# Three projections of a mixer and a cross attention: the last k-group of each pair of column blocks by seven products

## The chip, the cores and the metric

One program runs on one core of a Trainium2 chip. The metric is the device time of one execution in microseconds (us), the median of several runs. The engines are named as the profile names them: PE is TensorE (matmuls and transposes), DVE VectorE, ACT ScalarE, POOL GpSimd, and SP is SyncE, whose one queue issues the DMAs.

## What is computed

The input is 256 rows of width D = 2048 in fp32, which pass through two blocks. The first is a sliding-window attention and a gated feed-forward layer (FFN). The second block, where the change lies, is a hybrid mixer, a cross attention to 256 rows of memory, and an FFN with a short convolution, and then a last norm. Cut to the parts that matter:

```python
def hybrid_mixer(h, w_in, w_a2, b_a, g_gla, w_pool, pool_scale, w_branch, w_out):
    proj = h @ w_in                       # q, k, v, r, (gate rank 16), p, two gates of 2048
    ...
    o = gla_chunked(q, k, v, log_a)       # causal, with decays from the rank-16 gate
    ...
    o_gla = o.astype(h.dtype) * jax.nn.silu(r)
    o_pool = multiscale_pool(p, w_pool, pool_scale)
    y_gla = o_gla @ w_branch[:GLA_DV]
    y_pool = o_pool @ w_branch[GLA_DV:]
    gates = jax.nn.sigmoid(proj[..., OFF_G:])
    merged = gates[..., :D_MODEL] * y_gla + gates[..., D_MODEL:] * y_pool
    return merged @ w_out

def memory_cross_attention(h, mem_n, w_cq, w_ckv, w_co):
    q = (h @ w_cq).reshape(B, T, 4, 512)
    kv = (mem_n @ w_ckv).reshape(B, M, 2, 4, 512)
    s = jnp.einsum('bthd,bmhd->bhtm', q, k) * (512 ** -0.5)
    pr = jax.nn.softmax(s, axis=-1)
    return jnp.einsum('bhtm,bmhd->bthd', pr, v).reshape(B, T, D) @ w_co
```

Each of these products keeps nearly fp32 accuracy: a value x is split into a high part and the rest, and a product is the sum of three matmuls (high by high, high by low, low by high).

## The kernel before

**Tiles.** The activations lie transposed in SBUF in four groups of 512 channels, so one k-group is 4 slices of 128 channels by 256 rows, as a high and a low tile. The weights come in units of 512 by 512, 1 MB each, by one DMA on SP's queue (L215, four `raw` buffers). A unit is used as two *tasks*, each half of its rows: ACT casts the half into `wh` (L235), and DVE subtracts that from `raw` into `wl` (L236). There are five `wh` and five `wl` buffers, and `task()` lets the split run three tasks ahead of the matmuls. The order of all units is fixed by `plan()`. A `raw` buffer is loaded anew when the two tasks of its unit are split.

**Matmuls.** `gemm` walks over column blocks and k-groups. For one k and one of two row tiles t it issues the three matmuls of `mm` (L280 to L282), each 128 by 512, into one bank of PSUM. A pair of column blocks has four such banks (two blocks, two row tiles), and one k-group of it is 4 k x 2 blocks x 2 row tiles x 3 = 48 matmuls. PSUM has four banks `acc`, three `aux` and one `po`.

**Seven products.** The FFNs use `pair`, which does one k-group of a pair of blocks by seven products instead of eight: the 2 by 2 block of halves of the weights is combined by four additions on DVE (`form`, L252 to L256), the activations have sums made once, and each product is one task of 2 x 3 = 6 matmuls. A group is then 42 matmuls and seven tasks (seven casts on ACT, seven subtractions on DVE) instead of 48 and four. After the last group, eight additions on DVE and one copy on ACT put the results together, and between any two of the seven products `tick()` may let other work in.

**Order.** PE runs exactly in the order in which the code issues its work. The orders of DVE, ACT and SP are made by a scheduler, and each engine then works through its list from the front. Everything small (transposes, softmax, the GLA and pooling work) is written as generators, *jobs*: `spawn` starts one, `tick()`, called after each k of a `gemm`, steps each of them, and a `yield n` in a job makes it wait for n ticks. `need(job)` runs a job to its end at once. So a job's matmuls stand between those of the projections, some ticks behind the point where its input was made.

**The stages of the change.** The mixer projects 16 column blocks of `w_in`, in order q, k (`head_job`), then v, the pooling input (`pool_job`), r (`gla_out_job`), and then gates in turn with `w_br`. `gla_job` loads `w_a` for the rank-16 gate (L902), casts it (L904), multiplies (L917), and computes the GLA decays level by level on DVE (L955 to L971). `gla_out_job` takes a bank for each row tile, squares on ACT, a power on POOL (L445) and scales on DVE (L1026). In the cross attention, a job `memory` loads and norms the memory (squares at L1086) during the four blocks of `w_cq`. Then for each of four heads `w_ckv` gives K in one block and V in the next: `on_k` scales K (L436) and spawns a `group_job`, which three ticks later transposes it (L421) and splits the result (L403 on ACT, L404 on DVE). `on_v` scales V (L1102, L1103) and spawns `cross_job`, which does the scores, the softmax and the product with V. At its start stand the lines

```python
qT, kT = self.need(qT), self.need(kT)
S = self.bank((128, 2, 256))
```

Of the kernel before, what the change touches and what calls it, by code (L numbers as in the profile page):

```python
# [83 lines left out]
class _Net:  # L84
# [87 lines left out]
    def plan(self):  # L172

        p, U = [], self.units
        self.seven = set()

        def add(chunks, late=False):
            p.extend(chunks[c][g] for c, g in self.order(chunks, late))

        def pair(a, b, seven):  # L180
            for g in range(len(a)):
                if g in seven:
                    self.seven.add(len(p))
# [15 lines left out]
        add([U("w_in", n) for n in (0, 1)], True)  # L199
        add([U("w_in", n) for n in (2, 3, 6, 7, 4, 5)])  # L200
        for ns in BRANCH:
            add([U("w_in", 8 + 4 * j + n) for n in ns for j in range(2)])
            add([U("w_br", n, (2 * j, 2 * j + 1)) for n in ns for j in range(2)])
        add([U("w_out", n) for n in range(4)], True)
        add([U("w_cq", n) for n in range(4)], True)
        add([U("w_ckv", 4 * j + h) for h in range(4) for j in range(2)])
# [94 lines left out]
    def differences(self, acts, seven):  # L301


        nc = self.nc
        out = []
        for g, z in enumerate(acts):
            h, l = z = self.need(z)
            f = self.s4([128, 4, 256])
            nc.vector.tensor_add(f, h.bitcast(F32), l.bitcast(F32))
            p, q = f[:, :, 0:128], f[:, :, 128:256]  # L310
            yield 2
            if g not in seven:
                h, l = (self.s2([128, 4, 128], F32R) for _ in range(2))
                nc.vector.tensor_sub(p, p, q)
                nc.scalar.copy(h, p)
                nc.vector.tensor_sub(l, p, h.bitcast(F32))
            else:
                s = self.s4([128, 8, 128])
                nc.vector.tensor_add(s[:, 0:2], q[:, 0:2], q[:, 2:4])
                nc.vector.tensor_sub(s[:, 2:4], s[:, 0:2], p[:, 0:2])  # L320
                nc.vector.tensor_sub(s[:, 4:6], p[:, 0:2], q[:, 0:2])
                nc.vector.tensor_sub(s[:, 6:8], p[:, 2:4], s[:, 2:4])
                yield 1
                h, l = (self.s4([128, 8, 128], F32R) for _ in range(2))
                nc.scalar.copy(h, s)
                nc.vector.tensor_sub(l, s, h.bitcast(F32))
            out.append((h, l))
            yield 2
        return out

    def pair(self, left, right, acts, diffs, seven):
# [18 lines left out]
        o1 = None  # L350
        for g in range(len(acts)):
# [14 lines left out]
            end = g == seven[-1]  # L366
            product(p3, S, 6, 0, end)
            product(o1, A, 0, 0, end)
# [4 lines left out]
            if end:  # L373
                add(a, p2, u)
                yield a
            product(o6, S, 2, 0, end)
            if end:
                add(u, o6, u)
            product(p5, S, 0, 0, end)
# [4 lines left out]
            product(o7, S, 4, 0, end)  # L384
            if end:
# [440 lines left out]
    def mixer(self):  # L826
# [4 lines left out]

        def proj(c, done):
            return (self.units("w_in", c), done)

        def head_job(pss, sc):

            rows = self.scaled(pss, sc)
            yield 4
            dst = self.s4([128, 2, 4, 128])
            for t in range(2):  # L840
                b = self.bank((128, 4, 128))
                for h in range(4):
                    nc.tensor.transpose(b[:, h], rows[t][:, h * 128:h * 128 + 128], self.ident)
                nc.scalar.copy(dst[:, t], b)
                yield 1
            return dst

        qk = []
        self.gemm([proj(0, lambda p: qk.append(self.spawn(head_job(p, rq)))),
                   proj(1, lambda p: qk.append(self.spawn(head_job(p, r))))], xacts, late=True)  # L850
        gla = self.spawn(self.gla_job(xacts, r, qk))
# [8 lines left out]
        def on_r(p):  # L860
            t = self.s4([128, 2, 512])
            for i in range(2):
# [4 lines left out]

        self.gemm([proj(2 + c, on_v) for c in range(2)], xacts)
        self.gemm([proj(6 + c, lambda p, c=c: pacts.append(self.spawn(self.pool_job(c, p, r)))) for c in range(2)],
                  xacts)  # L870
        self.gemm([proj(4 + c, on_r) for c in range(2)], xacts)

        macts, gates = [], {}

        def on_gate(p, n, j):
            for t in range(2):
                s = gates[n, j, t] = self.s2([128, 512])
                nc.scalar.activation(s, p[t], AF.Sigmoid, scale=r[:, t:t + 1])

# [8 lines left out]
        for ns in BRANCH:  # L888
            self.gemm([proj(8 + 4 * j + n, lambda p, n=n, j=j: on_gate(p, n, j))
                       for n in ns for j in range(2)], xacts)  # L890
            for n in ns:
# [5 lines left out]
    def gla_job(self, xacts, r, qk):  # L897
# [22 lines left out]
        aT = self.s2([32, 256])  # L920
        nc.vector.tensor_copy(aT, pa)
        yield 1
        bT = self.s4([128, 2, 4, 128])
        z, e = self.s4([128, 2, 512]), self.s4([128, 2, 512])
        for t in range(2):
            pz = self.bank()
            nc.tensor.matmul(pz, aT[:, t * 128:t * 128 + 128], wa2, start=True, stop=True)
            nc.vector.scalar_tensor_tensor(z[:, t], pz, r[:, t:t + 1], ba, op0=ALU.mult, op1=ALU.add)

        nc.scalar.activation(e, z, AF.Abs)  # L930
# [5 lines left out]
        for t in range(2):  # L936
            b = self.bank((128, 4, 128))
            for h in range(4):
                nc.tensor.matmul(b[:, h], z[:, t, h * 128:h * 128 + 128], self.tri, start=True, stop=True)
            nc.scalar.copy(bT[:, t], b)  # L940
            yield 1
        qT, kT = (self.need(z) for z in qk)
# [60 lines left out]
    def gla_out_job(self, c, gla, v, sr):  # L1003
# [5 lines left out]
        for t in range(2):  # L1009
# [18 lines left out]
            og.append(o)  # L1028
            yield 1
        hl = yield from self.group_job(og, self.gains("g_gla_2", c))  # L1030
        return hl

    def pool_job(self, c, pss, r):
# [19 lines left out]
        for g in range(2):
            b = self.bank((128, 2, 256))
            for dt in range(2):
                for ct in range(2):
                    nc.tensor.matmul(b[:, dt], wpl[:, g, ct, dt * 128:dt * 128 + 128], pooled[:, g, ct],
                                     start=ct == 0, stop=ct == 1)
            self.split(hl, 2 * g, b, self.gains("pool_scale_2", c))
            yield 1  # L1060
        return hl


    def cross(self):
# [7 lines left out]
        def memory():  # L1072
# [7 lines left out]
            for t in range(2):  # L1080
# [4 lines left out]
                for i, raw in enumerate(raws):  # L1085
# [4 lines left out]
        rm = self.spawn(memory())  # L1090
        self.gemm([(self.units("w_cq", n),
                    lambda p: qT.append(self.spawn(self.group_job(self.scaled(p, rq))))) for n in range(4)], xacts, late=True)
        rm = self.need(rm)

        def on_k(p):
            kT.append(self.spawn(self.group_job(self.scaled(p, rm))))
# [10 lines left out]

        self.gemm([(self.units("w_ckv", 4 * j + h), f)
                   for h in range(4) for j, f in enumerate((on_k, on_v))], macts)
        self.residual("w_co", range(4), oacts, "g_ffn_2", late=True)  # L1110

    def cross_job(self, qT, kT, v):
# [3 lines left out]
        for t in range(2):  # L1116
            for k in range(4):
                self.mm(S[:, t], qT, k, t, [z[:, k] for z in kT], k == 0, k == 3)
            yield 1
        mx, den = self.sm([128, 2]), self.sm([128, 2])  # L1120
# [5 lines left out]
        for t in range(2):  # L1126
            nc.vector.tensor_scalar(p[:, t], p[:, t], den[:, t:t + 1], None, op0=ALU.mult)
        yield 3
        b = self.bank((128, 2, 256))
# [3 lines left out]
        pt = self.s2([128, 2, 256], F32R), self.s2([128, 2, 256], F32R)  # L1133
        self.split(pt, 0, b)
        yield 2
        hl = self.group()
        for k in (0, 2):
            b = self.bank((128, 2, 256))
            for j in range(2):
                for m in range(2):  # L1140
                    self.mm(b[:, j], v, m, k + j, [z[:, m] for z in pt], m == 0, m == 1)
            self.split(hl, k, b)
            yield 1
        return hl
# [187 lines left out]
```

## Time and profile before

| | |
|---|---|
| time before, median of 3 runs | 2688.29 us (2687.02 to 2688.56) |
| the profiled execution: its own time | 2686.66 us |
| its span in the trace | 2684.5 us |
| busy: PE, DVE, ACT | 2657.9, 1890.7, 1424.2 us |
| granted clock, mean over the span | 0.999 |
| first loads of w_in, w_br, w_out | at 954.5, 1220.8 and 1440.2 us |
| first loads of w_cq, w_ckv, w_co | at 1531.0, 1623.3 and 1819.5 us |
| K and V of the first head scaled | at 1672.37 and 1695.01 us |

The span is the time from the first to the last record, and the profiled execution's own time is 2.2 us longer. All times in rows are counted from the span's start. A matmul's record (0.39 us) is longer than the distance to the next one, since they overlap. So the distance of starts is what one costs.

### The profile page before, as it was taken

To read this page: it belongs to the slowest core of one execution; us is meant where nothing else is said; L and a number is where in the kernel's file an instruction comes from. 1 tells how busy PE (TensorE), PEld (TensorE's weight loads), DVE (VectorE), ACT (ScalarE), POOL (GpSimd) and SP (SyncE) were. 2 spreads that over 40 slices of the span, in tenths; PEclk is the share of its full clock that TensorE was granted. 3 is DMA by queue.
4 is the path that set the end of the run, shared out by engine and by line. 5 is a ranking of instruction groups with operands and counts; after the bars stand their busy time and mean duration, and the time that the engine had idled before them with its cause. 6 is when DMAs were issued, how large, how long until landed. Compare 5 with 4: busy or idle time off the path is not lost.

```text
span 2684.5 us, 31592 instructions
## 1 busy us (share of the span) xinstructions
PE 2657.9 (99%) x12352; PEld 2195.2 (82%) x12352; DVE 1890.7 (70%) x2225; ACT 1424.2 (53%) x1849; POOL 27.1 (1%) x27
## 2 busy tenths in 40 slices
PE   8999999999999999999999999999999999999998
PEld 7778888888888888888888888888878888888887
DVE  7775799888888864655545555454578877777776
ACT  6555555555555555454444555444555655555554
POOL 0100000000000000000000000000000000000000
PEclk9999999999999999999999999999999999999999
DMA  7334455555555554445555566444554555555553
GB/s 304 113 126 145 169 218 187 205 192 206 209 195 200 194 187 178 151 172 188 188 190 193 183 225 212 172 157 168 183 180 175 190 193 194 192 190 195 194 193 138
DMA packets 74086, 499.61 MB, mean 186 GB/s; under 512 B 8496, under 2 KB 9392, under 8 KB 14928
## 3 DMA queue, kind: packets, MB, share of 16 engines
q1 hardware_dynamic: 73936, 497.59, 51.4%
q8 instruction: 97, 1.59, 0.2%
q14 instruction: 53, 0.43, 0.0%
HBM read 495.46 MB, written 2.10 MB: 185 GB/s over the span
## 4 chain that ended last, share of the span: by engine, by line
PE 97%; DVE 2%; ACT 1%; POOL 0%; DMA 0%; issue 0%; SPq 0%; POOLq 0%; DVEq 0%; ACTq 0%
PE acc L280 29%; PE acc L282 29%; PE acc L281 29%; PE aux L421 2%; PE aux L282 1%; PE aux L281 1%; PE aux L280 1%; PE po L734 1%; PE po L282 1%; PE po L281 1%; PE po L280 1%; PE aux L969 0%; POOL sm L445 0%; DVE wl L236 0%; DMA raw<-in_w_qkv 0%; PE aux L695 0%
## 5 line engine op out<-in xcount | busy, mean ns | idle before, releaser
L236 DVE TENSOR_TENSOR wl<-raw,wh 128x1024 fp32r<-128x1024 f32 (+1 forms) x1012 | 1230.7, 1220 | 689.0 <-ACT wh L235 677.1
L235 ACT CAST wh<-raw 128x1024 fp32r<-128x1024 f32 (+1 forms) x1012 | 1060.2, 1051 | 1084.0 <-PE acc L282 1020.6
L280 PE MATMUL acc<-wh,s 128*128 128x512 f32 x3440 | 1364.1, 397 | 7.4 <-ACT wh L235 5.5
L282 PE MATMUL acc<-wh,s 128*128 128x512 f32 x3440 | 1342.6, 390 | 0.6 <-DVE s L404 0.6
L281 PE MATMUL acc<-wl,s 128*128 128x512 f32 x3440 | 1341.0, 390 | 0.4 <-DVE wl L236 0.4
L280 PEld LDWEIGHTS acc<-wh,s 128*128 128x128 f32 x3440 | 646.9, 188 | 145.5 <-DVE s L382 7.1
L282 PEld LDWEIGHTS acc<-wh,s 128*128 128x128 f32 x3440 | 646.2, 188 | 138.1 <-DVE s L404 1.1
L281 PEld LDWEIGHTS acc<-wl,s 128*128 128x128 f32 x3440 | 647.3, 188 | 128.2 <-DVE wl L236 1.7
L467 DVE TENSOR_TENSOR x<-acc,x 128x512 f32<-128x512 f32 x112 | 72.8, 682 | 0.0
L421 PEld LDWEIGHTS aux<-con,s 128*128 128x128 f32 x408 | 50.2, 140 | 15.7 <-issue 4.0
L421 PE MATMUL aux<-con,s 128*128 128x128 f32 x408 | 60.9, 272 | 1.8 <-DVE s L1162 1.8
L1159 ACT ACTIVATE s<-aux,vec 128x256 f32<-128x256 f32 x88 | 47.9, 560 | 12.5 <-PE aux L421 7.8
L403 ACT CAST s<-aux 128x512 fp32r<-128x512 f32 x66 | 38.4, 584 | 28.9 <-PE aux L421 18.6
L445 POOL TENSOR_TENSOR sm<-sm,mhalf 128x2 f32<-128x2 f32 (+3 forms) x22 | 26.0, 1182 | 2651.0 <-DVE sm L453 2314.1
L404 DVE TENSOR_TENSOR s<-aux,s 128x512 fp32r<-128x512 f32 x66 | 44.6, 687 | 11.5 <-ACT s L403 10.3
L408 ACT ACTIVATE s<-aux,vec 128x256 fp32r<-128x256 f32 x80 | 37.7, 473 | 22.3 <-PE aux L421 14.2
L280 PE MATMUL aux<-wh,s 128*128 128x512 f32 x120 | 46.7, 389 | 0.0
L281 PE MATMUL aux<-wl,s 128*128 128x512 f32 x120 | 46.7, 389 | 0.0
L282 PE MATMUL aux<-wh,s 128*128 128x512 f32 x120 | 46.7, 389 | 0.0
L409 DVE SCALAR_TENSOR_TENSOR s<-aux,vec,s 128x256 fp32r<-128x256 f32 x80 | 38.3, 482 | 6.5 <-ACT s L408 5.3
L1160 DVE SCALAR_TENSOR_TENSOR s<-aux,vec,s 128x255 f32<-128x255 f32 x88 | 41.0, 478 | 2.4 <-ACT s L1159 0.2
L1162 DVE SCALAR_TENSOR_TENSOR s<-aux,vec,s 128x254 f32<-128x254 f32 x88 | 40.0, 477 | 1.1
(195 smaller groups left out, 1309.1 us busy)
## 6 DMA issues: line engine op xcount, KB each, us to landing
raw<-in_w_up SPq DMA_DIRECT2D x132, 1024.0 KB, 4.8
raw<-in_w_dn SPq DMA_DIRECT2D x88, 1024.0 KB, 4.8
raw<-in_w_in SPq DMA_DIRECT2D x64, 1024.0 KB, 4.8
raw<-in_w_gate SPq DMA_DIRECT2D x44, 1024.0 KB, 4.8
raw<-in_w_ckv SPq DMA_DIRECT2D x32, 1024.0 KB, 4.7
raw<-in_w_qkv SPq DMA_DIRECT2D x19, 1024.0 KB, 5.4
raw<-in_w_o SPq DMA_DIRECT2D x16, 1024.0 KB, 4.7
raw<-in_w_br SPq DMA_DIRECT2D x16, 1024.0 KB, 4.7
```

Source lines behind the costliest of these rows:

```text
L235: nc.scalar.copy(h[:, m], raw[:, m])
L236: nc.vector.tensor_sub(l[:, m], raw[:, m], h[:, m].bitcast(F32))
L280: nc.tensor.matmul(o, ah[:, k, s], h, start=first, stop=False)
L281: nc.tensor.matmul(o, ah[:, k, s], l, start=False, stop=False)
L282: nc.tensor.matmul(o, al[:, k, s], h, start=False, stop=last)
L403: nc.scalar.copy(h[:, k0:k0 + n], src)
L404: nc.vector.tensor_sub(l[:, k0:k0 + n], src, h[:, k0:k0 + n].bitcast(F32))
L421: self.nc.tensor.transpose(b[:, j, t * 128:t * 128 + 128], srcs[t][:, (k + j) * 128:(k + j) * 128 + 128], self.ident)
L467: nc.vector.tensor_add(xs[t], pss[t], xs[t])
L1159: nc.scalar.activation(y[:, j], b[:, j], AF.Identity, bias=bb, scale=w2)
L1160: nc.vector.scalar_tensor_tensor(y[:, j, 1:256], b[:, j, 0:255], w1, y[:, j, 1:256], op0=ALU.mult, op1=ALU.add)
L1162: nc.vector.scalar_tensor_tensor(y[:, j, 2:256], b[:, j, 0:254], w0, y[:, j, 2:256], op0=ALU.mult, op1=ALU.add)
```

## The change

The 14 pairs of column blocks of `w_in` (8 pairs), `w_cq` (2) and `w_ckv` (4) no longer go through `gemm` but through a new `pair8`: three k-groups as before, into four `acc` banks, and the fourth by seven products. Four of these go into `acc` banks, and four banks of their own (three `aux`, one `po`) take the others. No `tick()` stands between the seven products, so no job's work does either. The sums of the activations' last group are made by a new job `sums_job`. Some waits of jobs are longer (`head_job` 8 ticks, `pool_job` 9, the `group_job` of Q and K in the cross attention 8), gates and scaled results are written in place, and `on_k` and `on_v` of a head are now called one right behind the other, at the end of the pair.

```diff
+        for n in (0, 2, 6, 4):
+            pair(U("w_in", n), U("w_in", n + 1), (3,))
...
+        for h in range(4):
+            pair(U("w_ckv", h), U("w_ckv", 4 + h), (3,))
...
+    def pair8(self, left, right, acts, sums):
...
+        c11, c21, c22, c12 = (self.bank(tag="acc") for _ in range(4))
+        for g in range(3):
+            acts[g] = z = self.need(acts[g])
+            for units, outs in ((right, (c12, c22)), (left, (c11, c21))):
+                for k, w in enumerate(self.weights(units[g])):
+                    for t in range(2):
+                        self.mm(outs[t], z, k, t, w, g == 0 and k == 0, g == 2 and k == 3 and outs[t] is c22)
+                    self.tick()
+        acts[3] = A = self.need(acts[3])
+        S = self.need(sums)
...
+        o1, o6, o7, o5 = (self.bank(tag=z) for z in ("aux", "aux", "aux", "po"))
+        u, a, b, c = (self.s2([128, 512]) for _ in range(4))
+        product(c12, S[1], 2, 0)
+        product(o1, A, 0, 0, True)
+        nc.scalar.copy(u, o1)
+        product(c11, A, 2, 0)
+        add(a, c11, u)
+        yield a
+        product(o6, S[0], 2, 0, True)
+        add(u, o6, u)
+        product(o5, S[0], 0, 0, True)
+        add(b, o5, u)
+        add(b, c12, b)
+        yield b
+        product(o7, S[1], 0, 0, True)
+        add(u, o7, u)
+        product(c21, A, 2, 1)
+        add(c, c21, u)
+        yield c
+        add(u, o5, u)
+        add(u, c22, u)
+        yield u
...
-        self.gemm([(self.units("w_ckv", 4 * j + h), f)
-                   for h in range(4) for j, f in enumerate((on_k, on_v))], macts)
+        for h in range(4):
+            k, v = self.pairs8(self.units("w_ckv", h), self.units("w_ckv", 4 + h), macts, sums)
+            on_k(k)
+            on_v(v)
```

Of K, the halves are `a` and `c`, of V `b` and `u`. The first place to look at is on PE, at the end of the first head's K. Before, these were the rows (`acc` is V's bank, `con` the identity, so the `aux` rows are transposes of K; L280 to L282 are the three matmuls):

```order
L421 MATMUL aux_12780<-con,s_2433_12755 128x128
L280 MATMUL acc_12758<-wh_12720,s_2303_12077 128x512
L281 MATMUL acc_12758<-wl_12721,s_2303_12077 128x512 [waits DVE_49]
L282 MATMUL acc_12758<-wh_12720,s_2304_12078 128x512
L280 MATMUL acc_12759<-wh_12720,s_2303_12077 128x512
L281 MATMUL acc_12759<-wl_12721,s_2303_12077 128x512
L282 MATMUL acc_12759<-wh_12720,s_2304_12078 128x512
L421 MATMUL aux_12797<-con,s_2432_12754 128x128 [waits PE_49]
L421 MATMUL aux_12797<-con,s_2433_12755 128x128
```

K's transposes stand there between matmuls of V's block, and the scores only behind that block. In the changed kernel, at the end of the first head's pair (its last product, then the transposes L499, then the scores, whose lines L283 to L285 are those of `mm`):

```order
L284 MATMUL acc_12855<-wl_13150,s_2478_12630 128x512
L285 MATMUL acc_12855<-wh_13149,s_2479_12631 128x512
L499 MATMUL aux_13212<-con,s_2578_13113 128x128 [waits Activation_49]
L499 MATMUL aux_13212<-con,s_2580_13115 128x128 [waits Activation_49]
L499 MATMUL aux_13212<-con,s_2578_13113 128x128
L499 MATMUL aux_13212<-con,s_2580_13115 128x128
L499 MATMUL aux_13219<-con,s_2578_13113 128x128 [waits DVE_49]
L499 MATMUL aux_13219<-con,s_2580_13115 128x128
L499 MATMUL aux_13219<-con,s_2578_13113 128x128
L499 MATMUL aux_13219<-con,s_2580_13115 128x128
L283 MATMUL aux_13226<-s_2600_13210,s_2458_12532 128x256 [waits DVE_49,Activation_49]
L284 MATMUL aux_13226<-s_2601_13211,s_2458_12532 128x256 [waits DVE_49]
```

The transposes and the scores now follow the last product with nothing between, and the next pair comes behind them. On DVE, the rows at the same place are these (L396 to L401 are the last additions of `pair8`, L398 makes `c`, L239 are subtractions `wl`, L1194 those of V, L482 the splits of K's transposes). Before, the splits stood behind one another with no addition ahead:

```order
L236 TENSOR_TENSOR wl_12788<-raw_12656,wh_12787 128x1024 [waits DMAHW3_49,PE_49,Activation_49]
L236 TENSOR_TENSOR wl_12811<-raw_12656,wh_12810 128x1024 [waits Activation_49]
L404 TENSOR_TENSOR s_2440_12779<-aux_12780,s_2439_12778 128x512 [waits Activation_49]
L404 TENSOR_TENSOR s_2440_12779<-aux_12797,s_2439_12778 128x512 [waits Activation_49]
L236 TENSOR_TENSOR wl_12829<-raw_12690,wh_12828 128x1024 [waits DMAHW4_49,Activation_49]
```

And now:

```order
L396 TENSOR_TENSOR s_2577_13112<-aux_13110,s_2577_13112 128x512 [waits PE_49]
L239 TENSOR_TENSOR wl_13190<-raw_13043,wh_13189 128x1024 [waits DMAHW6_49,Activation_49]
L398 TENSOR_TENSOR s_2580_13115<-acc_12855,s_2577_13112 128x512 [waits DVE_49,PE_49]
L1194 SCALAR_TENSOR_TENSOR s_2599_13205<-s_2579_13114,sm_12852,s_2598_13204 128x512 [waits Activation_49,Pool_49]
L400 TENSOR_TENSOR s_2577_13112<-po_13111,s_2577_13112 128x512 [waits DVE_49]
L239 TENSOR_TENSOR wl_13265<-raw_13043,wh_13264 128x1024
L401 TENSOR_TENSOR s_2577_13112<-acc_12856,s_2577_13112 128x512 [waits DVE_49]
L482 TENSOR_TENSOR s_2601_13211<-aux_13212,s_2600_13210 128x512 [waits Activation_49]
L482 TENSOR_TENSOR s_2601_13211<-aux_13219,s_2600_13210 128x512 [waits Activation_49]
L1194 SCALAR_TENSOR_TENSOR s_2599_13205<-s_2577_13112,sm_12852,s_2598_13204 128x512 [waits Activation_49]
L239 TENSOR_TENSOR wl_13283<-raw_13153,wh_13282 128x1024 [waits DMAHW7_49]
```

The first split, L482, has five instructions between it and the addition that makes `c`. On ACT, the rows between the end of the pair and the split of K are, in this order: a cast into `wh` that waits for the pair's last product, V's first half, K's second half scaled, and the two casts of K's transposes. The last place is SP's list at the start of the mixer. Before:

```order
L215 DMA raw_8044<-in_w_in 128x2048 [waits DMAHW3_49,DVE_49]
L215 DMA raw_8082<-in_w_in 128x2048 [waits DMAHW4_49,DVE_49]
L912 DMA s_1599_8139<-in_lmask 128x1024 [waits PE_49]
L902 DMA s_1595_8129<-in_w_a 128x256
L215 DMA raw_8147<-in_w_in 128x2048 [waits DMAHW5_49,DVE_49]
```

And now:

```order
L218 DMA raw_8097<-in_w_in 128x2048 [waits DMAHW2_49,DVE_49]
L218 DMA raw_8099<-in_w_in 128x2048 [waits DMAHW3_49,DVE_49]
L218 DMA raw_8124<-in_w_in 128x2048 [waits DMAHW5_49,DVE_49]
L218 DMA raw_8174<-in_w_in 128x2048 [waits DMAHW6_49,DVE_49]
L984 DMA s_1610_8154<-in_w_a 128x256
```

The load of `w_a` stood behind that of `lmask`. Now `lmask` is loaded earlier, and right ahead of `w_a` stand four loads of `raw`, each of which waits until DVE has split what its buffer held. The matmuls with `w_a` (L917) begin 5 ticks after `gla_job` was started. Before, transposes of `head_job` stood in these ticks too, and now, with its wait of 8, only the 30 matmuls of the next pair do.

## Rows read from the trace of the kernel before

**Rows 1.** the page: busy time, and the chain that ended last by engine

```profile
PE 2657.9 (99%) x12352; PEld 2195.2 (82%) x12352; DVE 1890.7 (70%) x2225; ACT 1424.2 (53%) x1849; POOL 27.1 (1%) x27
PE 97%; DVE 2%; ACT 1%; POOL 0%; DMA 0%; issue 0%; SPq 0%; POOLq 0%; DVEq 0%; ACTq 0%
```

**Rows 2.** the waits of PE, longest first: us in total, times, longest

```profile
PE acc L280 <- ACT wh L235: 5.5, 1, 5.5
```

**Rows 3.** the costliest groups: count, busy us, mean ns, idle before

```profile
L236 DVE TENSOR_TENSOR wl<-raw,wh 128x1024 fp32r<-128x1024 f32 (+1 forms) x1012 | 1230.7, 1220 | 689.0 <-ACT wh L235 677.1
L235 ACT CAST wh<-raw 128x1024 fp32r<-128x1024 f32 (+1 forms) x1012 | 1060.2, 1051 | 1084.0 <-PE acc L282 1020.6
```

**Rows 4.** timeline of PE, end of a conv-FFN pair: start us, us, line

```profile
2030.03 0.39 PE L282 MATMUL acc<-wh,s 128*128 128x512 f32 x1
...
2036.14 0.39 PE L282 MATMUL acc<-wh,s 128*128 128x512 f32 x1
2036.47 0.50 PE L280 MATMUL acc<-wh,s 128*128 128x512 f32 x1
2036.81 0.39 PE L281 MATMUL acc<-wl,s 128*128 128x512 f32 x1
```

**Rows 5.** timeline of DVE around the end of the same pair

```profile
2027.51 2.58 DVE L236 TENSOR_TENSOR wl<-raw,wh 128x1024 fp32r<-128x1024 f32 x2 [1.22 <-ACT wh L235]
...
2030.52 0.69 DVE L374 TENSOR_TENSOR s<-acc,s 128x512 f32<-128x512 f32 x1 [0.43 <-PE acc L282]
...
2036.93 1.22 DVE L236 TENSOR_TENSOR wl<-raw,wh 128x1024 fp32r<-128x1024 f32 x1
2038.06 0.69 DVE L388 TENSOR_TENSOR s<-acc,s 128x512 f32<-128x512 f32 x1
2038.66 1.22 DVE L236 TENSOR_TENSOR wl<-raw,wh 128x1024 fp32r<-128x1024 f32 x1
```

**Rows 6.** timeline of ACT, K of the first head scaled

```profile
1672.37 1.31 ACT L436 ACTIVATE s<-acc,sm 128x512 f32<-128x512 f32 x2 [1.05 <-PE acc L282]
```

**Rows 7.** timeline of PE, the first transposes of that K

```profile
1675.52 0.60 PE L421 MATMUL aux<-con,s 128*128 128x128 f32 x4
1675.87 0.48 PE L280 MATMUL acc<-wh,s 128*128 128x512 f32 x1
```

**Rows 8.** groups by line between 1623 and 1825 us

```profile
L404 DVE TENSOR_TENSOR s<-aux,s 128x512 fp32r<-128x512 f32 x19 | 12.9, 687 | 6.9 <-ACT s L403 5.7 <-PE acc L281 1.2
L403 ACT CAST s<-aux 128x512 fp32r<-128x512 f32 x19 | 11.1, 584 | 11.4 <-PE aux L282 7.7 <-PE aux L421 3.7
L1103 DVE SCALAR_TENSOR_TENSOR s<-acc,sm,s 128x512 fp32r<-128x512 f32 x6 | 4.3, 749 | 1.4 <-ACT s L1102 1.4
```

**Rows 9.** DMA issues by line: xcount, KB each, median us to landing

```profile
s<-in_w_a SPq DMA_DIRECT2D x1, 128.0 KB, 5.6
```

**Rows 10.** timeline of ACT, the cast of w_a

```profile
1031.77 0.41 ACT L904 CAST s<-s 128x256 fp32r<-128x256 f32 x1
```

**Rows 11.** groups by line between 1060 and 1130 us

```profile
L955 DVE TENSOR_TENSOR s<-s 128x512 f32<-128x512 f32 x14 | 9.6, 685 | 0.0
L971 DVE COPY_PREDICATED s<-s,aux 128x256 f32<-128x256 int32 x14 | 7.3, 519 | 1.7 <-PE aux L969 1.7
L959 DVE TENSOR_TENSOR s<-s,s 128x256 f32<-128x256 f32 x14 | 5.9, 424 | 0.9 <-ACT s L957 0.9
```

**Rows 12.** groups by line between 1120 and 1220 us

```profile
L1026 DVE SCALAR_TENSOR_TENSOR s<-aux,sm,s 128x256 f32<-128x256 f32 x8 | 3.5, 480 | 3.3 <-POOL sm L445 3.3
L445 POOL TENSOR_TENSOR sm<-sm,mhalf 128x2 f32<-128x2 f32 x4 | 2.8, 696 | 216.2 <-DVE sm L1020 216.2
```

**Rows 13.** timeline of ACT near the end of the query projection

```profile
1617.61 0.63 ACT L1086 ACTIVATE s<-s 128x512 f32<-128x512 f32 x1 [1.80 <-DMA s<-in_mem]
```

**Rows 14.** stretches: busy of PE, PEld, DVE, ACT, POOL; PEclk; DMA, GB/s

```profile
2670.00:2684.50 14.50, 5.79 (x26) 4.47 (x24) 5.09 (x12) 2.89 (x6) 1.10 (x2) 0.86 0.38 145
1980.00:2005.00 25.00, 22.56 (x105) 17.82 (x105) 16.68 (x27) 17.39 (x25) 0.00 (x0) 1.00 0.43 154
```

More of the change, by code (lines that the diff above doesn't have):

```diff
@@ L317, in differences @@
             else:
[L318 to L326, printed above, removed]
+                out.append((yield from self.four_sums(p, q)))
+                continue
             out.append((h, l))
@@ L329, in differences, with four_sums @@
         return out
+    def four_sums(self, p, q, small=False):
+        nc = self.nc
+        s = self.s4([128, 8, 128])
+        nc.vector.tensor_add(s[:, 0:2], q[:, 0:2], q[:, 2:4])
+        nc.vector.tensor_sub(s[:, 2:4], s[:, 0:2], p[:, 0:2])
+        nc.vector.tensor_sub(s[:, 4:6], p[:, 0:2], q[:, 0:2])
+        nc.vector.tensor_sub(s[:, 6:8], p[:, 2:4], s[:, 2:4])
+        yield 1
+        if small:
+            out = []
+            for z in (s[:, 0:4], s[:, 4:8]):
+                h, l = (self.s2([128, 4, 128], F32R) for _ in range(2))
+                nc.scalar.copy(h, z)
+                nc.vector.tensor_sub(l, z, h.bitcast(F32))
+                out.append((h, l))
+            return out
+        h, l = (self.s4([128, 8, 128], F32R) for _ in range(2))
+        nc.scalar.copy(h, s)
+        nc.vector.tensor_sub(l, s, h.bitcast(F32))
+        return [(h[:, z], l[:, z]) for z in (slice(0, 4), slice(4, 8))]
@@ new lines, in sums_job, with product @@
+    def sums_job(self, acts, small=False):
+        while len(acts) < 4 or not isinstance(acts[3], tuple) and not acts[3].done:
+            yield 2
+        h, l = self.need(acts[3])
+        f = self.s4([128, 4, 256])
+        self.nc.vector.tensor_add(f, h.bitcast(F32), l.bitcast(F32))
+        yield 2
+        return (yield from self.four_sums(f[:, :, 0:128], f[:, :, 128:256], small))
+    def pair8(self, left, right, acts, sums):
+        nc = self.nc
+        add = nc.vector.tensor_add
+        c11, c21, c22, c12 = (self.bank(tag="acc") for _ in range(4))
[8 more added lines that the diff above has]
+        S = self.need(sums)
+        assert self.stream[self.used:self.used + 2] == [right[3], left[3]]
+        self.used += 2
+        def product(o, z, k, t, own=False):
+            h, l = self.task()
+            for i in range(2):
+                self.mm(o, z, k + i, t, (h[:, i], l[:, i]), own and i == 0, i == 1)
+        o1, o6, o7, o5 = (self.bank(tag=z) for z in ("aux", "aux", "aux", "po"))
[20 more added lines that the diff above has]
+        yield u
@@ L331, in pair, with pairs8 @@
+    def pairs8(self, left, right, acts, sums):
+        o = list(self.pair8(left, right, acts, sums))
+        return o[0::2], o[1::2]
     def pair(self, left, right, acts, diffs, seven):
@@ L366, in pair @@
             end = g == seven[-1]
-            product(p3, S, 6, 0, end)
+            product(p3, S[1], 2, 0, end)
             product(o1, A, 0, 0, end)
@@ L383, in pair @@
                 yield b
-            product(o7, S, 4, 0, end)
+            product(o7, S[1], 0, 0, end)
             if end:
@@ L866, in on_r @@
             gacts.append(self.spawn(self.gla_out_job(len(sr) - 1, gla, v, t)))
[L868 to L871, printed above, removed]
+        for p in proj(2):
+            on_v(p)
+        for c, p in enumerate(proj(6)):
+            pacts.append(self.spawn(self.pool_job(c, p, r)))
+        for p in proj(4):
+            on_r(p)
         macts, gates = [], {}
@@ L1028, in gla_out_job @@
             og.append(o)
+            del b
             yield 1
@@ L1134, in cross_job @@
         self.split(pt, 0, b)
+        del b
         yield 2
```

54 lines of the change are left out of this document (32 added, 22 removed).

## The prediction

> **What bounds the kernel now.** I read the page first: PE is busy for 2657.9 of 2684.5 us, and the chain that ended last is PE for 97% of the span [rows 1]. So what counts is how many matmuls PE issues, and each gap in which it waits. The waits of PE came next. The longest, 5.5 us, is at the start of the program [rows 2], and none of those listed lies in the stages that change, so every wait there after the change is new. The costliest groups give the prices of the split work: a `wl` on DVE 1.22 us, a `wh` on ACT 1.05 [rows 3].
>
> Then I looked for the place that already does what the change brings: the end of a pair in the conv FFN, which also closes with seven products. On PE 27 matmuls start in 2036.14 - 2030.03 = 6.11 us, 0.226 each. The first two starts of the next work come 0.33 and 0.34 apart, so that hand-over loses 0.2 us [rows 4]. DVE there idles 1.22 and 0.43 us ahead of the tail and is then packed without a gap: it runs behind PE. Call e the end of the pair's last matmul, 2036.14 + 0.39 = 2036.53. The addition that needs this product starts at 2038.06, e + 1.53, since a `wl` and earlier additions stand ahead of it [rows 5]. Steps of starts in a packed stretch: an addition 0.60, a `wl` 1.13. In the FFN nobody on PE waits for these additions at once. The change puts work behind them that PE does wait for.
>
> **The gain.** 14 pairs lose six matmuls each, 84 in all, 84 x 0.226 = -19.0 us [rows 4]. The Trainium skill, "TensorE: Matmul & The Clock Gate", section "Back-to-back issue gap", gives about 131 ns for 512 columns in a sustained stream, by which the gain would be an estimated 11.0 us and the sum 8 us worse. The trace does not agree: its step is 226 ns, and the sum goes by that.
>
> **What is added beside PE.** Each pair has three more tasks, four combinations and eight additions: on DVE 3 x 1.13 + 4 x 1.13 + 8 x 0.60 = 12.7 us, on ACT 3 x 1.05 and a copy. DVE is 70% busy, and the FFN carries the same load in such a group with 1.65 us of idle time left [rows 1, 5]. So the load itself costs nothing where no other work is on DVE, and I take the FFN's hand-over, 10 pairs x 0.2 = +2.0 us (0, or 10 x 1.13 = 11.3 where DVE is one `wl` later). The four pairs of `w_ckv` come apart from these.
>
> **The ends of the four K/V pairs.** Before, K was scaled at 1672.37, its transposes began at 1675.52, and PE filled the time with V's matmuls [rows 6, 7]. Now transposes and scores stand right behind the last product. On ACT the cast that waits for this product runs to e + 1.15, V's half follows to 1.8, and K's second half `c` is there at e + 2.2 and scaled by about e + 2.95. The transposes take to 3.6, and the first cast of them (0.58) to 4.25 [rows 7, 8]. But on DVE the first split stands behind `c` (start 1.53), V's half (0.66 from its 0.749), an addition (0.60), a `wl` (1.13) and an addition (0.60): it starts at e + 5.1 and, at 0.69, ends at 5.8 [rows 5, 8]. The second matmul of the scores needs it, so PE goes on at about e + 5.9. Useful in between are eight transposes (2 x 0.35) and one matmul, 0.8. The wait is 5.1 us, four times 20.4 us. Were DVE fully caught up at e, V's half would still wait for ACT until 1.8 and the split end at 5.5: 4.6 us each, 18.4. One more `wl` of delay gives 6.2, 25.
>
> **The mixer's start.** The loads ahead of `w_a` now wait for `wl`s behind the end of the first pair. By the DVE steps above, `wl` of the fourth task ends at e + 3.4; the load of `raw` and that of `w_a` issue at 3.8, and `w_a` lands 5.6 us later, at 9.4 [rows 9]. A cast of 0.41 [rows 10] and a subtraction of about as much bring e + 10.3. PE is there after 30 matmuls and the hand-over, e + 7.0: +3.3 (0 if the loads find their buffers free, 4.4 if one more `wl` stands ahead).
>
> **GLA beside the seven products.** In the tails of the pairs with v and with the pooling input DVE also holds GLA work in its list: 2 additions of 0.69 and 4 products of 0.42, 3.05 us, in the first; the same and 2 masked copies of 0.52, 4.1, in the second [rows 11]. Less the 1.65 that the FFN had to spare [rows 5], this makes `wl`s late by 1.4 and 2.45. In the second, the last level's query product stands 7.4 us of DVE steps behind `c` and ends at e + 9.6, when PE has been ready since 30 matmuls and 12 small ones, e + 8.4: 1.2 more. Together +5.1 (0, or 8.4 where none of that idle time is there).
>
> **The outputs of GLA.** Both `gla_out_job`s now start together, after the pair with r, and ask for four `aux` banks of three. The fourth waits until DVE has emptied the first: behind `c` at 1.53, three more additions, three scalings of r and a `wl` (7.1), POOL's power of 0.70, a `wl`, and two scalings of 0.48, to e + 9.2 [rows 8, 12]. PE arrives after 18 matmuls and eight half ones, e + 5.3: +3.9 (0, or 6.2 with two more `wl`s ahead).
>
> **The queries.** The squares of the memory waited 1.80 us for a DMA without PE seeing it [rows 13]. Now 48 ticks instead of 64 pass until then, and the squares stand on ACT ahead of the casts of the seven products: +1.8, the wait of that row (0, or 4.6 for two such waits and a cast of 1.05).
>
> **Sum.** -19.0 + 2.0 + 20.4 + 3.3 + 5.1 + 3.9 + 1.8 = +17.5 us. The profiled execution took 2686.66 us (span 2684.5), so 2704.2 for such a one. The median of the runs is 1.6 above the profiled one: 2705.8, rounded **2706**. About 0.2%, 5.4 us, is what a measurement here can tell from no change.
>
> **Rivals.**
> 1. *Not slower: the slack of DVE hides all but the K/V ends.* In the mixer and the queries DVE has more idle time than in the FFN, so the loads and jobs there come in time. Then -19.0 + 2.0 + 20.4 = +3.4, 2691.7, no change by 0.2%. With the K/V wait at its lower bound it is 2689.7. It decides when the summed other waits are under 2 us. For it speaks that the FFN loses only 0.2 per pair, against it that `w_a` and the four banks are chains of fixed steps and not a matter of DVE's load. Chance 0.15.
> 2. *Faster: the K/V chain is hidden too*, for instance because DVE's list leaves the split nearer to its cast than I read it: -17, 2671. Five instructions stand between `c` and the split, so 0.05.
> 3. *DVE bounds the tails.* Each of the ten other pairs loses a whole `wl`, 1.13: 11.3 in place of 2.0, 2715. For it speaks that no tick lies between the products, so that DVE gets no extra time from job matmuls; against it the FFN's idle 1.65. Chance 0.13.
> 4. *The clock falls in the new gaps.* In the last stretch of the trace PE was busy 5.79 of 14.5 us and the granted clock was 0.86, while 22.56 of 25 kept it at 1.00 [rows 14]. The first lost 0.14 x 14.5 = 2.0 us of full clock; the same at each of four K/V ends is +8, 2714. The Trainium skill, "TensorE: Matmul & The Clock Gate", Part 1, says that the gate passes half the pulses after PE has been idle and all of them after it has been busy; no gap as long as 5 us inside a stage is in this trace to show which it will be. Against it: a pair's 186 matmuls, 42 us, lie between two of these gaps. Chance 0.07.
>
> The forecast itself has 0.60. The range goes from 2690, where rival 1 is, to 2721, rival 3 with waits of the mixer near their upper ends: **2690 to 2721**. Faster by over 0.2% is rival 2 and the lowest edge of the first, 0.06. Within 0.2% (2683 to 2694) is most of rival 1, 0.15. Slower has the rest, 0.79.
>
> **What would show it.** In the changed profile 84 fewer matmuls of 128 x 512. Among PE's waits the longest in total should be the transposes for ACT and the scores for DVE's split, near 5 us at each of four places, over 42 us apart. After the first pair the matmuls with `w_a` should wait about 3 us for DVE, the last of four GLA banks about 4. PE busy should fall by some 19 us, and the chain should contain DVE and ACT at the K/V ends. The prediction is wrong if the K/V ends show under 3 us each, if the waits of the mixer add up to less than 5 or over 25, or if the step of 0.226 changes.

## The result and the profile after

The changed kernel takes 2714.3 us (median of 4 runs, 2712.2 to 2717.4), the one before 2688.4 beside it. The ratio is 1.0099, with a 95% interval of 1.0081 to 1.0116: slower by 1.0%, 26 us, where 2706 had been forecast with a range of 2690 to 2721. The profiled execution took 2712.2 us, with a span of 2710.4.

First the page of the changed kernel, busy time and the chain by engine, which answer to [rows 1]:

```profile
PE 2657.5 (98%) x12268; PEld 2189.5 (81%) x12268; DVE 2074.5 (77%) x2454; ACT 1477.3 (55%) x1909; POOL 28.8 (1%) x27
...
PE 92%; DVE 5%; issue 2%; ACT 1%; POOL 0%; DMA 0%; SPq 0%; DVEq 0%; POOLq 0%; ACTq 0%
```

PE has the 84 matmuls less (12268 for 12352), and is busy just as long: 2657.5 us for 2657.9. So its idle time has grown by about 26 us, and the 19 us that those matmuls took have come back as well, most of it as matmuls at a lower clock, as shown below. DVE is in the chain with 5% for 2% before. The waits of PE (us in total, times, longest), beside [rows 2]; before, none of these but the second was there:

```profile
PE aux L499 <- ACT s L514: 14.3, 4, 3.6
PE acc L283 <- ACT wh L238: 5.5, 1, 5.5
PE aux L284 <- DVE s L482: 3.6, 4, 1.2
...
PE aux L1101 <- DVE s L1111: 2.8, 1, 2.8
...
PE aux L999 <- DVE s L987: 2.7, 1, 2.7
PE aux L1061 <- DVE s L1082: 1.4, 1, 1.4
...
PE acc L283 <- DVE s L393: 1.2, 1, 1.2
```

L499 are K's transposes, waiting for K's scaled half, and L284 there is the second matmul of the scores, waiting for K's split. L1101 is the fourth bank of the GLA outputs, L999 the matmuls with `w_a`, L1061 the last GLA product, which waits for its query part, and the last row the first matmul of a pair that waits for the addition to `b`.

Where the time went, by the starts of the first matmul of each stage on PE's timeline, in us of the two profiled executions:

| stage | before | after | difference | saved matmuls | lost |
|---|---|---|---|---|---|
| w_in to the first w_br | 263.45 | 268.09 | +4.64 | -6.8 (5 pairs) | 11.4 |
| w_br and gates, to w_out | 220.42 | 217.61 | -2.81 | -4.1 (3 pairs) | 1.3 |
| w_cq | 90.79 | 88.23 | -2.56 | -2.7 (2 pairs) | 0.2 |
| w_ckv | 200.61 | 228.18 | +27.57 | -5.4 (4 pairs) | 33.0 |

All other stages together differ by -0.9 us. So the four K/V pairs make the result.

PE's timeline at the end of the first of them (start us, us, line):

```profile
1693.49 0.39 PE L285 MATMUL acc<-wh,s 128*128 128x512 f32 x1
1693.72 0.27 PE L499 MATMUL aux<-con,s 128*128 128x128 f32 x1
1697.57 1.75 PE L499 MATMUL aux<-con,s 128*128 128x128 f32 x7 [3.58 <-ACT s L514]
1699.15 0.58 PE L283 MATMUL aux<-s,s 128*128 128x256 f32 x1
1700.41 0.58 PE L284 MATMUL aux<-s,s 128*128 128x256 f32 x1 [0.68 <-DVE s L482]
...
1701.01 0.42 PE L283 MATMUL aux<-s,s 128*128 128x256 f32 x1
1701.22 0.41 PE L284 MATMUL aux<-s,s 128*128 128x256 f32 x1
...
1704.06 0.28 PE L284 MATMUL aux<-s,s 128*128 128x256 f32 x1
1704.18 0.28 PE L285 MATMUL aux<-s,s 128*128 128x256 f32 x1
...
1704.66 0.40 PE L283 MATMUL acc<-wh,s 128*128 128x512 f32 x1
```

Call e again the end of the pair's last matmul, 1693.49 + 0.39 = 1693.88. The second matmul of the scores, from which on PE runs without a wait, starts at 1700.41, e + 6.53, and it is e + 6.53 at the other three ends too. And there is a second thing: the scores start 0.21 us apart at first and 0.12 at the end. Granted clock and busy time in stretches of 2 us, in the columns of [rows 14]:

```profile
1694.00:1696.00 2.00, 0.00 (x0) 0.00 (x0) 2.00 (x3) 1.59 (x2) 0.00 (x0) 1.00 0.86 266
1696.00:1698.00 2.00, 0.43 (x2) 0.43 (x3) 2.00 (x5) 0.72 (x1) 0.00 (x0) 0.68 0.93 393
1698.00:1700.00 2.00, 1.73 (x8) 1.21 (x6) 2.00 (x4) 1.22 (x3) 0.00 (x0) 0.50 0.00 0
...
1704.00:1706.00 2.00, 2.00 (x13) 1.78 (x13) 0.69 (x1) 0.41 (x2) 0.00 (x0) 1.00 0.00 0
```

At this end the clock falls to half while PE waits (0.50 is 1.2 GHz), and stays there for several us after PE is back. It need not fall within the wait: at the third end, where PE resumes at 1811.27, it was still at 1.00 then and fell in the stretch behind:

```profile
1810.00:1812.00 2.00, 0.73 (x7) 0.73 (x7) 2.00 (x4) 0.87 (x2) 0.00 (x0) 1.00 0.86 360
1812.00:1814.00 2.00, 0.64 (x4) 0.20 (x2) 2.00 (x4) 1.44 (x3) 0.00 (x0) 0.70 0.26 33
1814.00:1816.00 2.00, 1.89 (x9) 1.89 (x10) 2.00 (x4) 0.21 (x1) 0.00 (x0) 0.50 0.84 295
```

Counted by the distances of starts over the whole w_ckv stage, steps with a wait lost 20.3 us (4.9, 5.3, 5.3 and 4.9 at the four ends), and slower steps 13.0, of which before had 1.2. Part of the slower steps are the transposes inside the wait, so the two numbers are not yet the prices of the chain and of the clock. An experiment below parts these.

The chain behind the wait is DVE's list, which answers to [rows 5]:

```profile
1693.75 0.68 DVE L393 TENSOR_TENSOR s<-acc,s 128x512 f32<-128x512 f32 x1
1694.35 0.68 DVE L396 TENSOR_TENSOR s<-aux,s 128x512 f32<-128x512 f32 x1
1694.95 1.21 DVE L239 TENSOR_TENSOR wl<-raw,wh 128x1024 fp32r<-128x1024 f32 x1
1696.08 0.68 DVE L398 TENSOR_TENSOR s<-acc,s 128x512 f32<-128x512 f32 x1
1696.68 0.74 DVE L1194 SCALAR_TENSOR_TENSOR s<-s,sm,s 128x512 fp32r<-128x512 f32 x1
1697.34 0.68 DVE L400 TENSOR_TENSOR s<-po,s 128x512 f32<-128x512 f32 x1
1697.94 1.21 DVE L239 TENSOR_TENSOR wl<-raw,wh 128x1024 fp32r<-128x1024 f32 x1
1699.08 0.68 DVE L401 TENSOR_TENSOR s<-acc,s 128x512 f32<-128x512 f32 x1
1699.68 1.27 DVE L482 TENSOR_TENSOR s<-aux,s 128x512 fp32r<-128x512 f32 x2
```

These rows follow one another without idle time. `c` (L398) starts at e + 2.2, one addition later than in the FFN, and the first split at e + 5.8. Between the two stand four instructions (a half of V, an addition, a `wl`, an addition), not five as was counted ahead of the result. On ACT, for [rows 6], K's second half waits for just this `c`, and the first cast of the transposes is done at 1699.10, 0.6 us before DVE comes to the split:

```profile
1696.80 0.72 ACT L514 ACTIVATE s<-s,sm 128x512 f32<-128x512 f32 x1 [1.21 <-DVE s L398]
1698.51 0.59 ACT L481 CAST s<-aux 128x512 fp32r<-128x512 f32 x1 [0.99 <-PE aux L499]
```

And the start of the mixer, for [rows 9, 10]: the load of `w_a` on SP, its cast on ACT, PE's matmuls.

```profile
1031.54 0.43 SPq L984 DMA_DIRECT2D s<-in_w_a  x1
...
1036.27 0.40 ACT L986 CAST s<-s 128x256 fp32r<-128x256 f32 x1 [1.73 <-DMA s<-in_w_a]
...
1037.18 1.27 PE L999 MATMUL aux<-s,s 128*32 128x256 f32 x8 [2.69 <-DVE s L987]
```

The load is issued at 1031.54, 3.7 us behind the end of the pair's last matmul, as forecast (3.8). From issue to cast it is 4.7 us, 0.9 less than the 5.6 of [rows 9]. PE too was there 0.3 earlier than forecast, so it waited 2.7 us instead of 3.3.

### The profile page after: what moved, and what is told of

Read it like the earlier page. It is cut to its first block, busy times and chain, and to the rows that moved or that the text cites. A ratio compares the mean times of both kernels' runs of the same rounds, so it can differ in the third digit from the quotient of the medians.

```text
span 2710.4 us, 31809 instructions
## 1 busy us (share of the span) xinstructions
PE 2657.5 (98%) x12268; PEld 2189.5 (81%) x12268; DVE 2074.5 (77%) x2454; ACT 1477.3 (55%) x1909; POOL 28.8 (1%) x27
## 4 chain that ended last, share of the span: by engine, by line
PE 92%; DVE 5%; issue 2%; ACT 1%; POOL 0%; DMA 0%; SPq 0%; DVEq 0%; POOLq 0%; ACTq 0%
PE acc L283 27%; PE acc L285 27%; PE acc L284 27%; PE aux L499 2%; PE aux L284 2%; PE aux L285 2%; PE aux L283 2%; DVE wl L239 1%; PE po L812 1%; PE po L284 1%; PE po L285 1%; PE po L283 1%; POOL sm L523 0%; PE aux L1054 0%; ACT wh L238 0%
## 5 line engine op out<-in xcount | busy, mean ns | idle before, releaser
L239 DVE TENSOR_TENSOR wl<-raw,wh 128x1024 fp32r<-128x1024 f32 (+1 forms) x1054 | 1279.1, 1218 | 525.4 <-ACT wh L238 511.7
L238 ACT CAST wh<-raw 128x1024 fp32r<-128x1024 f32 (+1 forms) x1054 | 1102.7, 1051 | 1043.8 <-PE acc L285 964.1
L283 PE MATMUL acc<-wh,s 128*128 128x512 f32 x3300 | 1309.6, 397 | 8.4 <-ACT wh L238 5.5
L285 PE MATMUL acc<-wh,s 128*128 128x512 f32 x3300 | 1288.3, 390 | 0.6 <-DVE s L482 0.6
L284 PE MATMUL acc<-wl,s 128*128 128x512 f32 x3300 | 1287.2, 390 | 0.4 <-DVE wl L239 0.4
L283 PEld LDWEIGHTS acc<-wh,s 128*128 128x128 f32 x3300 | 621.0, 188 | 146.2 <-DVE s L460 7.1
L285 PEld LDWEIGHTS acc<-wh,s 128*128 128x128 f32 x3300 | 620.3, 188 | 133.1 <-DVE s L482 1.1
L284 PEld LDWEIGHTS acc<-wl,s 128*128 128x128 f32 x3300 | 621.4, 188 | 122.7 <-DVE wl L239 1.4
L283 PE MATMUL aux<-wh,s 128*128 128x512 f32 x204 | 79.5, 390 | 0.0
L284 PE MATMUL aux<-wl,s 128*128 128x512 f32 x204 | 79.4, 389 | 0.0
L285 PE MATMUL aux<-wh,s 128*128 128x512 f32 x204 | 79.4, 389 | 0.0
L499 PE MATMUL aux<-con,s 128*128 128x128 f32 x408 | 62.5, 279 | 16.9 <-ACT s L514 14.3
L499 PEld LDWEIGHTS aux<-con,s 128*128 128x128 f32 x408 | 50.6, 143 | 31.1 <-ACT s L514 15.8
L256 DVE TENSOR_TENSOR raw<-raw,raw 128x1024 f32<-128x1024 f32 x44 | 53.9, 1225 | 1.4
L259 DVE TENSOR_TENSOR raw<-raw 128x1024 f32<-128x1024 f32 x44 | 53.9, 1224 | 1.4
L255 DVE TENSOR_TENSOR raw<-raw 128x1024 f32<-128x1024 f32 x44 | 53.8, 1224 | 1.4
L257 DVE TENSOR_TENSOR raw<-raw,raw 128x1024 f32<-128x1024 f32 x44 | 53.9, 1224 | 1.3
L482 DVE TENSOR_TENSOR s<-aux,s 128x512 fp32r<-128x512 f32 x66 | 44.1, 685 | 7.5 <-ACT s L481 7.1
```

The source lines that it names most:

```text
L238: nc.scalar.copy(h[:, m], raw[:, m])
L239: nc.vector.tensor_sub(l[:, m], raw[:, m], h[:, m].bitcast(F32))
L255: nc.vector.tensor_sub(b22, b22, b12)
L256: nc.vector.tensor_sub(b12, b12, b11)
L257: nc.vector.tensor_add(b11, b11, b22)
L259: nc.vector.tensor_sub(b21, b21, b11)
```

## The experiments

**The scores later.** The one added line lets K's job finish in the ticks of the next pair:

```diff
     def cross_job(self, qT, kT, v):
         nc = self.nc
+        yield 12
         qT, kT = self.need(qT), self.need(kT)
```

> The scores of a head wait 12 ticks into the next pair instead of standing right behind the pair's last product; all else as in the changed kernel. Theory (the K/V ends cost a wait of about 5.1 us each for K's way over ACT and DVE, and some 2 to 3 us each of half clock behind it): the waits of the transposes for ACT (14.3 us) and of the scores for DVE (3.6 us) go, the granted clock stays at 1.00 from 1650 to 1900 us, the w_ckv stage falls from 227.5 us to 196 to 199, and the time from 2714 to about 2684 us. Rival (DVE's added work is the cost, wherever it is waited for): the head's softmax and splits now meet the next tail, half of the loss comes back there as waits for wl, about 2698 us.

It took 2684.3 us (10 runs; ratio to before 0.9988, 0.9979 to 0.9997). The waits of the transposes for L514 and of the scores for L482 are gone, w_ckv takes 194.05 us, less than the 196 to 199 that were expected, and w_co 97.33 for 93.69, since the last head's scores are now in it. The clock over that stage, after the change and here (same columns as above):

```profile
1645.00:1895.00 250.00, 231.35 (x1081) 193.97 (x1080) 171.35 (x191) 122.54 (x152) 0.00 (x0) 0.94 0.44 159
```

```profile
1645.00:1845.00 200.00, 199.59 (x968) 166.64 (x967) 155.48 (x170) 112.52 (x137) 0.00 (x0) 1.00 0.48 176
```

One line gives back 30 us. But for that shift into w_co nothing of it returns elsewhere, so the loss was not DVE's load: DVE does the same work here.

**Filling the wait.** This parts the wait from the clock: the wait stays, but PE is kept busy in it.

```diff
             on_k(k)
+            z = self.need(macts[0])[0]
+            d = self.bank()
+            for i in range(14):
+                nc.tensor.matmul(d, z[:, 0, 0:128], z[:, 0:2, :], start=i == 0, stop=i == 13)
+            del d
             on_v(v)
```

> 14 useless matmuls of 128 x 512 (3.2 us at the step of 0.226) stand between the last product of each K/V pair and K's transposes, where PE waits 3.58 us for ACT; their result is read by nobody, and the chain through ACT and DVE is unchanged. Theory (part of the loss is the clock that falls in the gap): the granted clock stays at 1.00, the scores keep their step of 0.119 us, each K/V end is 2 to 3 us shorter though PE has 56 more matmuls to do, in all 2703 to 2706 us. Rival 1 (the clock costs nothing that the wait had not cost already): no change, 2714 us. Rival 2 (the filler delays K's transposes): later by up to 4 x 0.5, 2716 us.

It took 2708.0 us (5 runs, 2704.9 to 2708.7; ratio 1.0073, 1.0060 to 1.0085), 6.3 less than the changed kernel, with 56 matmuls more to do. PE's timeline at the same end:

```profile
1694.73 0.39 PE L285 MATMUL acc<-wh,s 128*128 128x512 f32 x1
1694.96 3.34 PE L1205 MATMUL aux<-s 128*128 128x512 f32 x14
...
1698.82 0.98 PE L499 MATMUL aux<-con,s 128*128 128x128 f32 x7 [0.41 <-ACT s L514]
1700.04 0.38 PE L283 MATMUL aux<-s,s 128*128 128x256 f32 x1 [0.24 <-ACT s L481]
1701.66 0.38 PE L284 MATMUL aux<-s,s 128*128 128x256 f32 x1 [1.23 <-DVE s L482]
...
1702.00 0.28 PE L283 MATMUL aux<-s,s 128*128 128x256 f32 x1
1702.12 0.28 PE L284 MATMUL aux<-s,s 128*128 128x256 f32 x1
...
1704.51 0.40 PE L283 MATMUL acc<-wh,s 128*128 128x512 f32 x1
```

The scores now run 0.12 us apart from the start, and the granted clock is 1.00 over the stage:

```profile
1645.00:1890.00 245.00, 237.06 (x1152) 197.45 (x1152) 173.88 (x193) 124.36 (x154) 0.00 (x0) 1.00 0.45 163
```

The chain through DVE is untouched: the second matmul of the scores starts at 1701.66, e + 6.54 (e is 1695.12 here), for e + 6.53 without the filler, and so it is at all four ends. What changes lies behind it. From that matmul to the first one of the next pair it takes 2.85 us instead of 4.25. At the four ends the difference is 1.4, 2.0, 2.2 and 2.2 us, 7.9 in all. That is the whole gain of the w_ckv stage, which shrinks by 8.0 us in the profiled executions (220.14 for 228.18). So the half clock costs 8 us beside the wait. The median lies 2 us above the range that was expected.

**K and V as before.** `w_ckv` goes back to `gemm`, in the plan and in `cross`, with the shorter wait of K's job:

```diff
-        for h in range(4):
-            k, v = self.pairs8(self.units("w_ckv", h), self.units("w_ckv", 4 + h), macts, sums)
-            on_k(k)
-            on_v(v)
+        self.gemm([(self.units("w_ckv", 4 * j + h), f)
+                   for h in range(4) for j, f in enumerate((on_k, on_v))], macts)
```

> w_ckv goes back to the ordinary column blocks with K and V a block apart, as in the kernel before; w_in and w_cq keep the seven products. Theory: the w_ckv stage goes back from 227.5 to about 200.6 us and nothing else moves: 2714 - 27 = 2687 us, so that the ten other pairs together give back what they save (13.6 us) but for about 1. Rival (the ten others save their 13.6 us less 2, and the K/V stage hides a loss of other stages): 2677 us.

It took 2688.2 us (10 runs; ratio 1.0002, 0.9993 to 1.0011), no change. So the ten pairs of the mixer and the queries give back all of the 13.6 us that they save, and the whole loss of the change is in the K/V pairs. The w_ckv stage of this run is at 202.35 us, 1.7 above before, though it has the old order. Eight transposes of the queries (0.9 us) and a short wait ahead of them (0.5) now stand there; the transposes stood in w_cq before.

**The load earlier, the banks apart.**

```diff
+        wa = self.s2([128, 16, 16])
+        nc.sync.dma_start(wa, a["w_a"])
         qk = [self.spawn(head_job(p, z)) for p, z in zip(proj(0), (rq, r))]
-        gla = self.spawn(self.gla_job(xacts, r, qk))
+        gla = self.spawn(self.gla_job(xacts, r, qk, wa))
...
     def gla_out_job(self, c, gla, v, sr):
-        yield 2
+        yield 2 + 6 * c
```

> Two things in the mixer: the load of w_a is issued ahead of the first pair instead of behind it, and the second of the two jobs for the GLA outputs starts 6 ticks after the first. Theory: the waits for the cast of w_a (2.7 us, with about 1.7 us of lower clock behind it) and for the fourth bank (2.8 us) go, at most 0.5 us of the first is left: 2714 - 6.5 = about 2708 us. Rival (a late chain moves on): the matmul of the gate behind w_a or the outputs' way into w_br takes the wait over, 2712 to 2714 us.

It took 2708.8 us (5 runs, 2706.5 to 2709.8; ratio 1.0076, 1.0062 to 1.0090), 5.5 less than the changed kernel. The wait of L1101 is gone, and 0.86 of the 2.69 us at `w_a` is left, since its cast still stands where it did on ACT and DVE.

**All three together**, the scores later and the two of the mixer:

> The scores 12 ticks later, the load of w_a ahead of the first pair and the second GLA output job 6 ticks after the first, all together. Theory (the places are apart in time and do not touch each other): the two gains add, 2714.3 - 30.0 - 5.5 = about 2679 us, 0.3% under the kernel before. Rival (what is won in the mixer is lost at the next join, as the projections still end when the jobs do): 2684 us, as with the scores alone.

It took 2678.9 us (5 runs, 2676.7 to 2679.6; ratio 0.9967, 0.9954 to 0.9979). The places add. This version beats both kernels, by 0.3% and 1.3%.

**Two more ticks in GLA**, on top of that (`yield 6` ahead of the matmuls with `w_a`, `yield 5` ahead of the last product):

> The kernel with all three mends, and two more: the matmuls with w_a one tick later (6 instead of 5), and the last GLA product two ticks later (5 instead of 3). Theory: the 0.9 us wait for the cast of w_a and the 1.4 us wait for the last query product go, 2679 - 2.2 = 2677 us. Rival (the whole GLA chain is late by the same ticks where the outputs need it): 2679 us or above.

It took 2678.8 us (5 runs, 2674.7 to 2679.8; ratio 0.9965, 0.9953 to 0.9978): no gain. Both waits are gone from PE's list, and the wait for the addition to `b` has grown from 1.3 to 1.6. In the profiled executions the stage from w_in to w_br is only 0.5 us shorter, of the 2.2 that were expected. Where the rest went was not traced, and 2.2 us is hardly more than what these runs tell apart.

**Ticks between the products**, as the FFN's pairs have them:

```diff
                 self.mm(o, z, k + i, t, (h[:, i], l[:, i]), own and i == 0, i == 1)
+            self.tick()
```

> A tick after each of the seven products, as the FFN's pairs have it, so that other work may stand between them; all else as in the changed kernel. Theory (the loss sits at the ends of the K/V pairs, and K is only there after the last product): those waits stay within 1 us of 17.9, and the time within 2710 to 2718 us. Rival 1 (work left out between the products is what makes DVE late at their end): the K/V waits fall by a third and more, 2704 us or less. Rival 2 (jobs in the tail wait for the banks that the products hold): new waits of the small matmuls in w_in, 2720 us and more.

It took 2719.6 us (4 runs, 2717.7 to 2723.7; ratio 1.0118, 1.0102 to 1.0133), 5 us slower than the change and above the 2710 to 2718 that were expected. The K/V waits stay at 14.7 and 3.6 us, so the products without other work between are not their cause. The new waits are not where the second rival put them. They are these:

```profile
1091.69 0.51 PE L283 MATMUL acc<-wh,s 128*128 128x512 f32 x1 [2.00 <-DVE s L394]
...
1611.77 0.75 PE L283 MATMUL acc<-wh,s 128*128 128x512 f32 x1 [3.34 <-DVE s L394]
```

L394 is the second addition to `b`, which frees a bank for the next pair. On DVE more work stands ahead of it than in the changed kernel: at the first place products and masked copies of GLA, at the second not the jobs' work but four `wl`s in a row, where there was one.

```profile
1604.76 4.62 DVE L239 TENSOR_TENSOR wl<-raw,wh 128x1024 fp32r<-128x1024 f32 x4
```

Leaving other work out of the tail was a gain here.

**V behind the scores.** `cross_job` is spawned ahead of the two scalings of V in `on_v`:

> At a K/V end V is scaled behind the scores instead of ahead of them. In the lists of the engines V's half then leaves its place ahead of the first split of K on DVE, and a wl (1.13 us) takes that place, 0.47 us more than V's half (0.66); on ACT K's second half follows the cast directly. Theory (PE's second wait is DVE's list, step by step; the first is the addition that makes c): the transposes' wait for ACT stays at 14.3 us or falls by up to 1, the scores' wait for DVE rises from 3.6 by 4 x 0.5 to about 5.5 us, 2714 to 2718 us. Rival (ACT's list is the bound there): with V's half gone from ahead of K's the waits fall by 4 x 0.6, about 2712 us, and the scores' wait for DVE does not rise.

It took 2716.0 us (4 runs, 2714.6 to 2717.2; ratio 1.0107, 1.0093 to 1.0121). The time alone does not tell it from the changed kernel (2714.3); the waits do:

```profile
PE aux L499 <- ACT s L514: 14.3, 4, 3.6
PE aux L284 <- DVE s L482: 6.2, 4, 1.7
```

The first stays at 14.3, and the second rises from 3.6 to 6.2, somewhat more than the 5.5 that were expected. DVE's list at the first end has `c` at 1698.76 and the split at 1702.83, 4.07 us for the 3.60 after the change, the 0.47 that was worked out from the row that takes V's place. So DVE's list is the bound of that wait, and `c` that of the first.

## Why the prediction was right, and where it was off

The direction and the mechanism were right. The K/V ends make the result, PE waits there for DVE's list, the saved matmuls are there, and the removal of the forced order gives the time back. The forecast had PE go on at e + 5.9, which was 5.1 us of wait beside 0.8 of useful work, 20.4 in all. PE went on at e + 6.5 at each of the four ends, so in the forecast's own terms it is 5.7 each, 22.8 in all. The missing 0.6 is `c`, at e + 2.2 for 1.53. The 20.3 by steps with a wait looks like the forecast, but it leaves out the slow transposes within the wait. The lower bound of 4.6 us was a slip: a split that ends at 5.5 instead of 5.8 makes it 4.8.

The size was off by 8 us in the profiled execution (2712.2 for 2704.2). The mis-sized term is that of the K/V ends: the sum left the clock out, which was a rival of its own at 2714 with a chance of 0.07. It was wrong to hold it against the forecast: both happen together, the wait and then the half clock. The filled wait shows 7.9 us for it. The rival's price of 8 us came from the last stretch of the trace [rows 14], which is another place with another pattern of work, so that it fits so closely is luck. One sign that was named failed for the same reason: PE's busy time was to fall by 19 us and fell by 0.4.

The other terms, forecast and measured as PE's wait: `w_a` 3.3 and 2.7; the GLA outputs 3.9 and 2.8; the last query product 1.2 and 1.4. The `wl`s late beside GLA were put at 3.9, and no wait for `wl` of that kind is in the list: it shows as the 1.2 us for the addition to `b`. The queries' 1.8 did not come: the squares waited 0.95 and 0.70 us for DMAs on ACT, and no wait of PE goes back to them. In the table w_cq loses only 0.2 us, but some 1.4 of transposes and a wait moved from it into w_ckv. With the hand-overs (2.0) these terms had been put at 16.1 us for the ten pairs, and the table above has 12.9, or about 14.3 with what moved. That the total is off by just the price of the clock is luck too, since the chain (2.4 too little) and these terms (some 2 too much) nearly cancel.

Of the rivals, DVE as the bound of all tails (11.3 us over ten pairs) is out: the three pairs of the gates lose 1.3 us together. That slack hides everything but the K/V ends is out too: with the K/V pairs as before the time is that of the kernel before, 2688.2 us, where about 2677 would have been left. That the K/V chain is hidden did not come either.

Of the 19 us, the best version keeps 8.4 (2687.3 beside 2678.9). The rest was not traced to single places: in its profile w_in to w_br is at 262.2 us, 5.6 more than before less its saved matmuls.

## What to carry to other kernels

Here the saved matmuls paid only where nothing that PE waits for stood directly behind them. If a shorter product leaves its result to a chain over two other engines, let other PE work stand in between, by a tick count, as K's transposes had before. When a step moves, look at the list of the engine that comes after, since work behind it in the code may stand ahead of it there. And price a gap on PE with the clock: the wait and what the matmuls lose behind it add.

## What was not expected of the hardware

At the first of the K/V ends, with a gap on PE of 3.6 us, the granted clock was at 0.50 before the gap was over, and it was back at 1.00 about 6 us after PE had resumed. At the third, after a gap of the same length, it fell only when PE had resumed. Of two shorter gaps of nearly the same length, one had the clock fall and the other not. The stretches, in the columns as above, are that of the GLA outputs (a wait of 2.8 us) and that of `w_a` (2.7):

```profile
1198.00:1212.00 14.00, 11.18 (x50) 8.95 (x49) 12.82 (x20) 8.30 (x20) 3.11 (x2) 1.00 0.60 220
1034.00:1046.00 12.00, 9.30 (x48) 7.25 (x47) 3.39 (x4) 2.06 (x4) 0.00 (x0) 0.86 0.58 201
```

What decides between the two was not tried. And useless matmuls in a wait made the kernel faster: 56 of them, 14 in each of four waits, by 6.3 us.
